# Attention of a decoder trunk: two heads to a task, score products over 128 rows, value products of both heads in turn

## The chip, the cores and the metric

One core of a Trainium2 chip. The time is device microseconds of one execution; the kernel before has a median of 2147.78 us over three runs (2141.76 to 2147.9).

## What is computed

Two layers, each a half-step SwiGLU FFN, a mixer, a second FFN and a gated per-layer embedding, on 512 positions of 1024 features in f32. The mixer projects its input to q, k, v (8 heads of 64) and to the input of a state-space branch (SSM); attention and SSM outputs are normalised, joined and projected. Cut to the attention, with the three dilated windows as one masked softmax:

```python
proj = rms_norm(h, mix_pre_g[i]) @ w_in[i]
q, k, v, u = jnp.split(proj, [D_ATTN, 2 * D_ATTN, 3 * D_ATTN], axis=-1)
q, k = partial_rotary(q, positions), partial_rotary(k, positions)
attn = dilated_mixture_attention(q, k, v)     # per head: softmax(q k^T / 8 + mask) v
ssm = s5_mixer(u, ...)
mixed = jnp.concatenate([rms_norm(attn, attn_norm_g[i]), rms_norm(ssm, ssm_norm_g[i])], -1)
h = h + rms_norm(mixed @ w_out[i], mix_post_g[i])
```

The mask is the logarithm of the number of windows that hold a key (0, 1, 2 or 3), so that one softmax over the causal keys gives the mixture.

## The kernel before

Activations lie transposed (128 features on the partitions, 512 positions in a row). Dense products keep f32 precision with three float32r products each: weights and inputs are split into a high and a low part on ScalarE (a copy) and VectorE (a difference), and high*high, high*low, low*high are added in PSUM (`mm3`). Weights stream from HBM by SyncE's queue in units of up to 128x1024 words and are split just ahead of use.

The order of all instructions is fixed when the program is built. A planner (`Clock`) keeps a model of when each engine, tile and bank is free; generators (`spawn`) for attention, SSM lanes, weight splits and normalisations yield until their inputs are due, and whenever PE would have to wait, or between two steps of three dense products, the planner lets those that are due issue their instructions (`tick`). So each engine's queue is an interleaving; on the chip it is run strictly in that order. All PE products are recorded at line 562 (`mm`), transposes at 568 (`flip`), and the other engines' operations at 353. A tile named `sb_all`, `sr_all` or `z` is a large SBUF area cut into slots of 512 words (`sr_all` in float32r, 36 slots); `ps_all` is PSUM with 8 banks of 512 words.

The mixer (`mix`, lines 1732 to 1830) projects u and the first q/k pair, then v, starts two SSM lanes (`mixer`) and `attention`, projects the other q/k tiles while those run, then the SSM gate (`glu`), the SSM half of the output projection, and last, when attention is complete, the attention half (`finish`).

Attention goes over t = 0..3, a pair of heads each, since 128 partitions hold two heads of 64. `parts` (1663) makes from q and k of the pair: per head a tile with the high part of q on its own 64 partitions and the low part on the other 64, and a tile with the high part of k on both halves; and one tile `kl`, shared, with the low parts of k, each head's on its own half. Then for each block of 128 queries (qi = 3, 2, 1, 0) and each head, `head` (1620) is one task, at most LIVE = 6 at a time:

- two score products of W = 128 (qi + 1) keys into one PSUM bank: 128 rows (high and low q, high k) at line 1639 and 64 rows (high q, low k) at line 1640;
- VectorE adds the mask and takes the row maximum (a custom operation), ScalarE the exponential with its sum, VectorE a reciprocal and a scaling;
- qi + 1 transposes into a bank, and a copy to SBUF by ScalarE;
- qi + 1 value products with 64 weight columns, f32, into the head's half of the partitions of a bank that the eight tasks of t share (line 1658). On the chip an f32 product is two instructions, so four such products are eight records.

`attended` (1709) waits for the eight tasks, then scales and splits the result for `finish`.

Of the kernel before, what the change touches and what calls it, by code (L numbers as in the profile page):

```python
# [10 lines left out]
F32 = mybir.dt.float32  # L11
# [5 lines left out]
P = 128  # L17
SEQ = 512
# [33 lines left out]
LIVE = 6  # L52
# [683 lines left out]
class Trunk(Kernel):  # L736
# [886 lines left out]
    def head(self, M, t, hh, qi, bank):  # L1623

        v = M["v"]
        q, k, kl = (self.r(b) for b in M["parts"][t][hh])
        n = qi + 1
        W = n * P
        rows = slice(hh * HD, (hh + 1) * HD)
        yield self.ck.ready(q, k, kl[rows])  # L1630
        while len(self.sl.free) < 2:
            yield self.ck.after(200.0)
        p, pt = self.sl.get(), self.sl.get()
        st = self.o_st + 2 * (self.nst % 32)
        self.nst += 1
        m, den = self.w(st, 1), self.w(st + 1, 1)
        bk = yield from self.tbank()
        c = slice(qi * P, (qi + 1) * P)
        self.mm(self.pb(bk, W), q[:, c], k[:, 0:W], True, False)
        self.mm(self.pb(bk, W), q[rows, c], kl[rows, 0:W], False, True)  # L1640
        self.ve.tensor_tensor_reduce(
            out=self.b(p, W), in0=self.pb(bk, W), in1=self.w(self.o_const + C_MASK + SEQ - W, W), scale=-1.0,
            scalar=3e38, op0=ALU.add, op1=ALU.min, accum_out=m)
        self.free(bk)
        self.act(self.b(p, W), self.b(p, W), AF.Exp, scale=-1.0, bias=m, accum_out=den)
        yield self.ck.ready(self.b(p, W))
        self.ve.reciprocal(den, den)
        self.ts(self.b(p, W), self.b(p, W), den)
        yield self.ck.ready(self.b(p, W))
        bk = yield from self.tbank()  # L1650
        for j in range(n):
            self.flip(self.pb(bk, P, j * P), self.b(p)[:, j * P:(j + 1) * P])
        self.act(self.b(pt, W), self.pb(bk, W))
        self.free(bk)
        self.sl.put(p)
        yield self.ck.ready(self.b(pt, W))
        for j in range(n):
            self.mm(self.ps[rows, bank * SEQ + qi * P:bank * SEQ + (qi + 1) * P],
                    self.b(v[j])[:, t * P + hh * HD:t * P + (hh + 1) * HD], self.b(pt)[:, j * P:(j + 1) * P],
                    j == 0, j == n - 1)  # L1660
        self.sl.put(pt)
# [284 lines left out]
```

## Time and profile before

| | us |
|---|---|
| median of three runs | 2147.78 |
| the profiled execution's own time | 2144.88 |
| its span, first to last instruction | 2143.1 |
| PE busy | 2090.1 |
| VectorE busy | 1334.3 |
| ScalarE busy | 798.4 |

The two mixers' attention lies between 470 and 614 us and between 1533 and 1670 us of the span. Times in views are counted from the span's start. A matmul's length in a view is its modelled flight time; in a stream they overlap, so what one costs is the distance from its start to the next one's start. A merged row of the timeline shows the shape of its first instruction: the score rows at 525 and 604 hold 128-row and 64-row products in turn.

### The profile page before, as it was taken

How to read it: one execution, taken by the hardware profiler on the slowest of the kernel's cores; microseconds unless marked ns; L12 is line 12 of the kernel's file. 1: busy time of each engine (PE TensorE's matmuls, PEld its weight loads, DVE VectorE, ACT ScalarE, POOL GpSimd, SP SyncE). 2: the span in 40 equal slices, each digit the busy share in tenths (PEclk: the TensorE clock that was granted, in tenths of full speed). 3: DMA queues.
4: the chain of work that ended last, by engine and by line, in shares of the span. 5: the costliest groups of instructions: out<-in, count | busy, mean ns of one | idle time of the engine just before them, and what ended most of it. 6: DMA issues, size and time to landing. Idle time of an engine off the chain costs nothing.

```text
span 2143.1 us, 30766 instructions
## 1 busy us (share of the span) xinstructions
PE 2090.1 (98%) x11936; PEld 1780.0 (83%) x11936; DVE 1334.3 (62%) x2516; ACT 798.4 (37%) x1406; POOL 156.1 (7%) x167
## 2 busy tenths in 40 slices
PE   8999999989999999999999999998999999999997
PEld 7888888967789888889998888898777898888897
DVE  5887745776768975446674444467666864444474
ACT  4422333435554322223543222234356533222242
POOL 0000000101120000001200000011011200000022
PEclk9999999999999999999999999999999999999999
DMA  4424434471133534324324233246511333323131
GB/s 157 129 82 152 137 104 138 133 171 40 60 109 113 166 121 125 111 63 154 102 82 148 72 102 114 62 165 141 138 50 50 131 116 110 117 61 127 59 131 67
DMA packets 118145, 236.29 MB, mean 110 GB/s; under 512 B 27120, under 2 KB 58480, under 8 KB 118000
## 3 DMA queue, kind: packets, MB, share of 16 engines
q1 hardware_dynamic: 118000, 234.34, 35.3%
q8 instruction: 93, 1.52, 0.3%
q14 instruction: 52, 0.43, 0.1%
HBM read 208.60 MB, written 25.69 MB: 109 GB/s over the span
## 4 chain that ended last, share of the span: by engine, by line
PE 89%; DVE 6%; DMA 1%; issue 1%; ACT 1%; POOL 1%; SPq 0%; POOLq 0%; ACTq 0%; DVEq 0%
PE ps_all L562 88%; DVE sb_all L353 4%; DVE sr_all L353 2%; PE ps_all L568 1%; DMA sb_all<-scratch_t 1%; ACT sb_all L353 1%; POOL sb_all L353 1%; SPq L353 0%; ACT sr_all L353 0%; DVE z L353 0%; DMA sb_all<-weights 0%; DMA sb_all<-scratch_g 0%; DMA scratch_u<-sb_all 0%; ACT z L353 0%; POOLq L353 0%
## 5 line engine op out<-in xcount | busy, mean ns | idle before, releaser
L562 PE MATMUL ps_all<-sr_all 128*128 128x512 f32 (+2 forms) x7118 | 1447.2, 358 | 16.1 <-ACT sr_all L353 8.6
L562 PEld LDWEIGHTS ps_all<-sr_all 128*128 128x128 f32 (+1 forms) x7118 | 1185.1, 191 | 222.6 <-issue 19.2
L353 ACT ACTIVATE sr_all<-sb_all 128x512 fp32r<-128x512 f32 (+5 forms) x567 | 410.5, 742 | 562.7 <-DVE sb_all L353 398.9
L562 PE MATMUL ps_all<-sr_all,z 128*128 128x512 f32 (+1 forms) x2898 | 572.3, 348 | 0.9 <-DVE sr_all L353 0.9
L353 DVE TENSOR_TENSOR sr_all<-sb_all,sr_all 128x1024 fp32r<-128x1024 f32 (+5 forms) x455 | 417.8, 927 | 184.8 <-ACT sr_all L353 182.5
L562 PEld LDWEIGHTS ps_all<-sr_all,z 128*128 128x128 f32 x2898 | 469.8, 190 | 67.9 <-issue 1.8
L353 DVE TENSOR_TENSOR sb_all<-ps_all,sb_all 128x512 f32<-128x512 f32 (+1 forms) x396 | 244.4, 622 | 367.4 <-PE ps_all L562 361.7
L353 ACT ACTIVATE sb_all<-sb_all 128x256 f32<-128x256 f32 (+3 forms) x390 | 188.6, 490 | 483.2 <-DVE sb_all L353 481.1
L353 POOL TENSOR_TENSOR sb_all<-sb_all 128x256 f32<-128x256 f32 (+3 forms) x159 | 152.3, 960 | 1982.1 <-ACT sb_all L353 1739.1
L353 DVE TENSOR_TENSOR sb_all<-sb_all 128x256 f32<-128x256 f32 (+7 forms) x597 | 233.7, 407 | 22.6 <-DMA scratch_t<-sb_all 7.9
L353 ACT ACTIVATE sb_all<-ps_all 128x512 f32<-128x512 f32 (+5 forms) x228 | 102.9, 466 | 204.5 <-PE ps_all L562 166.8
L353 DVE SCALAR_TENSOR_TENSOR sb_all<-sb_all 128x512 f32<-128x512 f32 (+4 forms) x194 | 115.8, 599 | 65.0 <-ACT sb_all L353 63.3
L353 DVE TENSOR_TENSOR z<-sb_all,z 128x1024 fp32r<-128x1024 f32 (+2 forms) x112 | 120.2, 1075 | 55.3 <-ACT z L353 55.2
L562 PE MATMUL ps_all<-sb_all 128*64 128x128 f32 (+6 forms) x1412 | 127.4, 268 | 27.2 <-DMA sb_all<-scratch_t 12.6
L562 PEld LDWEIGHTS ps_all<-sb_all 128*64 128x64 f32 (+3 forms) x1412 | 108.1, 156 | 53.2 <-issue 27.1
L353 ACT ACTIVATE z<-sb_all 128x1024 fp32r<-128x1024 f32 (+2 forms) x112 | 103.5, 926 | 58.7 <-PE ps_all L562 39.2
L353 DVE TENSOR_SCALAR sb_all<-sb_all 128x32 f32<-128x32 f32 (+7 forms) x147 | 44.1, 306 | 37.3 <-POOL sb_all L353 20.7
L353 DVE SCALAR_TENSOR_TENSOR sb_all<-sb_all,ps_all 128x256 f32<-128x256 f32 x132 | 63.1, 480 | 4.3 <-PE ps_all L562 4.2
L353 DVE SCALAR_TENSOR_TENSOR sr_all<-sb_all,sr_all 128x256 fp32r<-128x256 f32 x96 | 51.8, 549 | 0.2 <-ACT sr_all L353 0.2
L353 DVE CUSTOM_DVE_ANT_0 sb_all<-ps_all,sb_all 128x512 f32<-128x512 f32 (+3 forms) x62 | 28.4, 485 | 34.5 <-PE ps_all L562 30.6
L568 PE MATMUL ps_all<-sb_all 128*128 128x128 f32 x218 | 33.9, 274 | 0.0
L568 PEld LDWEIGHTS ps_all<-sb_all 128*128 128x128 f32 x218 | 26.4, 140 | 7.3 <-issue 1.4
(38 smaller groups left out, 170.3 us busy)
## 6 DMA issues: line engine op xcount, KB each, us to landing
sb_all<-weights SPq DMA_DIRECT2D x263, 512.0 KB, 3.7
sb_all<-weights SPq DMA_DIRECT2D x96, 320.0 KB, 2.9
scratch_t<-sb_all SPq DMA_DIRECT2D x40, 256.0 KB, 3.2
scratch_h<-sb_all SPq DMA_DIRECT2D x80, 128.0 KB, 1.7
sb_all<-scratch_h SPq DMA_DIRECT2D x40, 256.0 KB, 5.8
sb_all<-scratch_t SPq DMA_DIRECT2D x16, 512.0 KB, 6.3
sb_all<-weights SPq DMA_DIRECT2D x32, 192.0 KB, 2.3
sb_all<-xt SPq DMA_DIRECT2D x16, 128.0 KB, 3.7
```

Of the source, the lines that this page charges most:

```text
L353: return f(*a, **k)
L562: self.nc.tensor.matmul(out, lhsT, rhs, start=start, stop=stop)
L568: self.nc.tensor.transpose(out, x, self.ident)
```

## The change

`head` becomes `block`, one task for both heads of a pair and one block of queries, LIVE = 3 of them at a time.

- The second score product runs over all 128 rows: `parts` now makes a low tile of k per head and copies it to the other half (two more copies on ScalarE for each t, and six `sr_all` slots in place of five), so the product holds also low q times low k.
- Where two heads' scores fit in one bank (qi = 0 and 1), they share it, as do their transposes, and one copy evacuates both; otherwise a task takes two banks and four slots.
- A value product of one head and one of the other stand in turn; their outputs are the two halves of the partitions of the same bank.
- The planner counts value products at half their former cost (`share` = 2).

```diff
@@ -49,7 +49,7 @@
 HEAD = 6
 PLE_HEAD = 4
 GLU_AT = 4
-LIVE = 6
+LIVE = 3
 LANES = ((0, 1), (2, 3))
 PREP_AT = 35000.0
@@ -1620,70 +1620,95 @@
         self.tt(dst, dst, self.b(b), ALU.add, eng=self.po)
         self.sl.put(b)
-    def head(self, M, t, hh, qi, bank):
+    def block(self, M, t, qi, bank):
         v = M["v"]
-        q, k, kl = (self.r(b) for b in M["parts"][t][hh])
+        parts = [[self.r(b) for b in x] for x in M["parts"][t]]
         n = qi + 1
         W = n * P
-        rows = slice(hh * HD, (hh + 1) * HD)
-        yield self.ck.ready(q, k, kl[rows])
-        while len(self.sl.free) < 2:
+        one = 2 * W <= SEQ
+        yield self.ck.ready(*[x for p in parts for x in p])
+        need = 2 if one else 4
+        while len(self.sl.free) < need:
             yield self.ck.after(200.0)
-        p, pt = self.sl.get(), self.sl.get()
-        st = self.o_st + 2 * (self.nst % 32)
-        self.nst += 1
-        m, den = self.w(st, 1), self.w(st + 1, 1)
-        bk = yield from self.tbank()
+        bufs = [self.sl.get() for _ in range(need)]
+        p = [self.b(bufs[0])[:, hh * W:(hh + 1) * W] if one else self.b(bufs[hh], W) for hh in range(2)]
+        pt = [self.b(bufs[1])[:, hh * W:(hh + 1) * W] if one else self.b(bufs[2 + hh], W) for hh in range(2)]
         c = slice(qi * P, (qi + 1) * P)
-        self.mm(self.pb(bk, W), q[:, c], k[:, 0:W], True, False)
-        self.mm(self.pb(bk, W), q[rows, c], kl[rows, 0:W], False, True)
-        self.ve.tensor_tensor_reduce(
-            out=self.b(p, W), in0=self.pb(bk, W), in1=self.w(self.o_const + C_MASK + SEQ - W, W), scale=-1.0,
-            scalar=3e38, op0=ALU.add, op1=ALU.min, accum_out=m)
-        self.free(bk)
-        self.act(self.b(p, W), self.b(p, W), AF.Exp, scale=-1.0, bias=m, accum_out=den)
-        yield self.ck.ready(self.b(p, W))
-        self.ve.reciprocal(den, den)
-        self.ts(self.b(p, W), self.b(p, W), den)
-        yield self.ck.ready(self.b(p, W))
-        bk = yield from self.tbank()
+        bks = []
+        sc = []
+        for hh in range(2):
+            if not (one and hh):
+                bks.append((yield from self.tbank()))
+            sc.append(self.pb(bks[-1], W, W * hh if one else 0))
+        for (q, k, kl), s in zip(parts, sc):
+            self.mm(s, q[:, c], k[:, 0:W], True, False)
+            self.mm(s, q[:, c], kl[:, 0:W], False, True)
+        dens = []
+        for hh in range(2):
+            st = self.o_st + 2 * (self.nst % 32)
+            self.nst += 1
+            m, den = self.w(st, 1), self.w(st + 1, 1)
+            dens.append(den)
+            self.ve.tensor_tensor_reduce(
+                out=p[hh], in0=sc[hh], in1=self.w(self.o_const + C_MASK + SEQ - W, W), scale=-1.0,
+                scalar=3e38, op0=ALU.add, op1=ALU.min, accum_out=m)
+            self.act(p[hh], p[hh], AF.Exp, scale=-1.0, bias=m, accum_out=den)
+        self.free(*bks)
+        for hh in range(2):
+            yield self.ck.ready(p[hh])
+            self.ve.reciprocal(dens[hh], dens[hh])
+            self.ts(p[hh], p[hh], dens[hh])
+        yield self.ck.ready(*p)
+        bks = []
+        for hh in range(2):
+            if not (one and hh):
+                bks.append((yield from self.tbank()))
+            for j in range(n):
+                self.flip(self.pb(bks[-1], P, (W * hh if one else 0) + j * P), p[hh][:, j * P:(j + 1) * P])
+            if not one:
+                self.act(pt[hh], self.pb(bks[-1], W))
+        if one:
+            self.act(self.b(bufs[1], 2 * W), self.pb(bks[0], 2 * W))
+        self.free(*bks)
+        self.sl.put(*bufs[:need // 2])
+        yield self.ck.ready(*pt)
         for j in range(n):
-            self.flip(self.pb(bk, P, j * P), self.b(p)[:, j * P:(j + 1) * P])
-        self.act(self.b(pt, W), self.pb(bk, W))
-        self.free(bk)
-        self.sl.put(p)
-        yield self.ck.ready(self.b(pt, W))
-        for j in range(n):
-            self.mm(self.ps[rows, bank * SEQ + qi * P:bank * SEQ + (qi + 1) * P],
-                    self.b(v[j])[:, t * P + hh * HD:t * P + (hh + 1) * HD], self.b(pt)[:, j * P:(j + 1) * P],
-                    j == 0, j == n - 1)
-        self.sl.put(pt)
+            for hh in range(2):
+                rows = slice(hh * HD, (hh + 1) * HD)
+                self.mm(self.ps[rows, bank * SEQ + qi * P:bank * SEQ + (qi + 1) * P],
+                        self.b(v[j])[:, t * P + hh * HD:t * P + (hh + 1) * HD], pt[hh][:, j * P:(j + 1) * P],
+                        j == 0, j == n - 1, 2)
+        self.sl.put(*bufs[need // 2:])
     def parts(self, M, t):
         q, k = self.b(M["q"][t]), self.b(M["k"][t])
-        got = yield from self.rs.tgets(1, 1, 1, 1, 1)
-        kl = self.r(got[4])
-        heads = [(self.r(got[2 * hh]), self.r(got[2 * hh + 1])) + tuple(
+        got = yield from self.rs.tgets(1, 1, 1, 1, 1, 1)
+        heads = [tuple(self.r(g) for g in got[3 * hh:3 * hh + 3]) + tuple(
             slice(g * HD, (g + 1) * HD) for g in (hh, 1 - hh)) for hh in range(2)]
         yield self.ck.written(q)
-        for a, _, own, _ in heads:
+        for a, _, _, own, _ in heads:
             self.act(a[own], q[own])
-        yield max(self.ck.written(a[own]) for a, _, own, _ in heads)
-        for a, _, own, other in heads:
+        yield max(self.ck.written(a[own]) for a, _, _, own, _ in heads)
+        for a, _, _, own, other in heads:
             self.tt(a[other], q[own], a[own].bitcast(F32), ALU.subtract)
         yield self.ck.written(k)
-        for _, b, own, _ in heads:
+        for _, b, _, own, _ in heads:
             self.act(b[own], k[own])
-        yield max(self.ck.written(b[own]) for _, b, own, _ in heads)
-        for _, b, own, other in heads:
-            self.tt(kl[own], k[own], b[own].bitcast(F32), ALU.subtract)
+        yield max(self.ck.written(b[own]) for _, b, _, own, _ in heads)
+        for _, b, l, own, other in heads:
+            self.tt(l[own], k[own], b[own].bitcast(F32), ALU.subtract)
             self.act(b[other], k[own])
+        yield max(self.ck.written(l[own]) for _, _, l, own, _ in heads)
+        for _, _, l, own, other in heads:
+            self.act(l[other], l[own].bitcast(F32))
         self.sl.put(M["q"][t], M["k"][t])
         M["rs"][t] = got
-        M["parts"][t] = [(got[2 * hh], got[2 * hh + 1], got[4]) for hh in range(2)]
+        M["parts"][t] = [tuple(got[3 * hh:3 * hh + 3]) for hh in range(2)]
     def attention(self, i, M):
@@ -1695,13 +1720,12 @@
             bank = yield from self.tbank()
             mine = []
             for qi in range(3, -1, -1):
-                for hh in range(2):
-                    while sum(not d[0] for d in live) >= LIVE:
-                        yield self.ck.after(100.0)
-                    d = self.ck.spawn(self.head(M, t, hh, qi, bank))
-                    live.append(d)
-                    mine.append(d)
-                    live = [d for d in live if not d[0]]
+                while sum(not d[0] for d in live) >= LIVE:
+                    yield self.ck.after(100.0)
+                d = self.ck.spawn(self.block(M, t, qi, bank))
+                live.append(d)
+                mine.append(d)
+                live = [d for d in live if not d[0]]
             ends.append(self.ck.spawn(self.attended(i, t, M, bank, mine)))
         while not all(d[0] for d in ends):
             yield self.ck.after(100.0)
```

What that makes of PE's order is shown at three places of the first mixer. In names, `sr_all` products 128x512, 128x384, 128x256 and 128x128 are dense or score products by their width (64x128 is a value or mixer product with 64 weight columns; L568 a transpose).

The scores of t = 2, behind the SSM gate's products. Before:

```order
L562 MATMUL ps_all<-sr_all 128x512 x45
L562 MATMUL ps_all<-sr_all,z_4015 128x512 x3
L562 MATMUL ps_all<-sr_all 128x512 x2
L562 MATMUL ps_all<-sr_all 128x384 x2
L562 MATMUL ps_all<-sr_all 128x256 x2
L562 MATMUL ps_all<-sr_all 128x512 x2
L562 MATMUL ps_all<-sr_all 128x384 x2
L562 MATMUL ps_all<-sr_all 128x256 x2
L562 MATMUL ps_all<-sr_all,z_4015 128x512 x15
```

and now:

```order
L562 MATMUL ps_all<-sr_all 128x512 x45
L562 MATMUL ps_all<-sr_all,z_4007 128x512 x18
L562 MATMUL ps_all<-sr_all 128x512 x4
L562 MATMUL ps_all<-sr_all 128x384 x4
L562 MATMUL ps_all<-sr_all 128x256 x4
L562 MATMUL ps_all<-sr_all,z_4007 128x512 x9
```

Each head's scores of the first three blocks were a row of their own (x2: one 128-row and one 64-row product); now both heads' four products stand together.

Value products at t = 0, where one head's tiles lie in `z`. Before:

```order
L568 MATMUL ps_all<-sb_all,z_3362 128x128 x3
L562 MATMUL ps_all<-sr_all 128x256 x2
L562 MATMUL ps_all<-z_3362,sb_all 64x128 x4
L562 MATMUL ps_all<-sr_all 128x128 x2
L562 MATMUL ps_all<-sr_all 128x512 x3
```

and now:

```order
L562 MATMUL ps_all<-sb_all 64x128
L562 MATMUL ps_all<-z_3362,sb_all 64x128
L562 MATMUL ps_all<-sb_all 64x128
L562 MATMUL ps_all<-z_3362,sb_all 64x128 x5
L562 MATMUL ps_all<-sr_all 128x512 x3
L562 MATMUL ps_all<-sr_all 128x128 x4
```

Four products of one head in a row have become products of two heads in turn.

The end of attention, ahead of the attention half of the output projection (128x256). Before:

```order
L562 MATMUL ps_all<-sr_all 128x128 x2
L562 MATMUL ps_all<-sr_all,z_4015 128x512 x3
L568 MATMUL ps_all<-sb_all 128x128 x2
L562 MATMUL ps_all<-sr_all,z_4015 128x512 x3
L568 MATMUL ps_all<-sb_all 128x128 x2
L562 MATMUL ps_all<-sr_all,z_4015 128x512 x3
L568 MATMUL ps_all<-sb_all 128x128
L562 MATMUL ps_all<-sr_all,z_4015 128x512 x3
L562 MATMUL ps_all<-sb_all 64x128 x2
L568 MATMUL ps_all<-sb_all 128x128
L562 MATMUL ps_all<-sb_all 64x128 x4
L562 MATMUL ps_all<-sr_all 128x256 x21
```

and now:

```order
L562 MATMUL ps_all<-sb_all 64x128 x8
L562 MATMUL ps_all<-sr_all 128x256 x4
L562 MATMUL ps_all<-sb_all 64x128 x6
L562 MATMUL ps_all<-sr_all,z_4007 128x512 x3
L562 MATMUL ps_all<-sr_all 128x128 x4
L568 MATMUL ps_all<-sb_all 128x128 x6
L562 MATMUL ps_all<-sb_all 64x128 x6
L562 MATMUL ps_all<-sr_all 128x256 x18
```

Before, four times three dense products stood between the last scores (128x128 x2) and the last value products; now the last scores are followed directly by the last transposes.

## Rows read from the trace of the kernel before

**Rows 1.** Span and mean granted TensorE clock of the one core.
```profile
core 0: 2143.1 us, clock 0.988
```

**Rows 2.** Part 1 of the page: busy time, share of the span, instructions.
```profile
PE 2090.1 (98%) x11936; PEld 1780.0 (83%) x11936; DVE 1334.3 (62%) x2516; ACT 798.4 (37%) x1406; POOL 156.1 (7%) x167
```

**Rows 3.** Part 4 of the page: the chain that ended last, by engine.
```profile
PE 89%; DVE 6%; DMA 1%; issue 1%; ACT 1%; POOL 1%; SPq 0%; POOLq 0%; ACTq 0%; DVEq 0%
```

**Rows 4.** Busy time by stretch: us, engines' busy (instructions), clock, DMA share, GB/s.
```profile
470.00:541.00 71.00, 68.24 (x483) 50.33 (x480) 48.96 (x117) 37.57 (x77) 10.76 (x7) 0.95 0.18 49
541.00:569.00 28.00, 27.74 (x134) 20.54 (x133) 23.23 (x37) 14.77 (x28) 4.66 (x3) 1.00 0.15 48
569.00:614.00 45.00, 44.11 (x237) 32.19 (x238) 26.39 (x77) 29.36 (x69) 3.50 (x3) 1.00 0.22 71
...
1620.00:1670.00 50.00, 50.00 (x252) 36.58 (x251) 31.28 (x83) 32.63 (x75) 6.51 (x4) 0.97 0.17 54
```

**Rows 5.** Group by line, engine, shape: the 64-row product of the widest score.
```profile
L562 PE MATMUL ps_all<-sr_all 64*128 64x512 f32 x16 | 8.2, 514 | 0.0
```

**Rows 6.** Score products on PE: start us, us, engine, line, form, count.
```profile
525.12 4.41 PE L562 MATMUL ps_all<-sr_all 128*128 128x512 f32 x12
529.46 0.74 PE L562 MATMUL ps_all<-sr_all,z 128*128 128x512 f32 x2
...
604.45 0.58 PE L562 MATMUL ps_all<-sr_all 128*128 128x128 f32 x2
604.96 0.96 PE L562 MATMUL ps_all<-sr_all,z 128*128 128x512 f32 x3
```

**Rows 7.** Dense products on PE, undisturbed stretches.
```profile
514.13 10.48 PE L562 MATMUL ps_all<-sr_all 128*128 128x512 f32 x45
524.44 0.85 PE L562 MATMUL ps_all<-sr_all,z 128*128 128x512 f32 x3
...
659.59 4.48 PE L562 MATMUL ps_all<-sr_all 128*128 128x256 f32 x36
```

**Rows 8.** Products with 64 weight columns on PE: mixer (465), values (580, 1638).
```profile
465.22 1.09 PE L562 MATMUL ps_all<-sb_all 128*64 128x128 f32 x16
466.25 0.98 PE L562 MATMUL ps_all<-sb_all,z 64*64 64x128 f32 x14
...
580.52 1.09 PE L562 MATMUL ps_all<-sb_all 128*64 128x128 f32 x8
581.54 0.44 PE L568 MATMUL ps_all<-sb_all 128*128 128x128 f32 x2
...
1638.97 2.18 PE L562 MATMUL ps_all<-sb_all 128*64 128x128 f32 x18
1641.08 0.96 PE L562 MATMUL ps_all<-sr_all 128*128 128x512 f32 x3
1641.97 1.20 PE L562 MATMUL ps_all<-sb_all 128*64 128x128 f32 x9
```

**Rows 9.** Group on ScalarE by shape: copies of half a q or k.
```profile
L353 ACT ACTIVATE sr_all<-sb_all 64x512 fp32r<-64x512 f32 x48 | 30.1, 627 | 16.2 <-POOL sb_all L353 15.6
```

**Rows 10.** VectorE: first and last step of one head's 128-column softmax.
```profile
607.33 0.29 DVE L353 CUSTOM_DVE_ANT_0 sb_all<-ps_all,sb_all 128x128 f32<-128x128 f32 x1
...
608.64 0.29 DVE L353 TENSOR_SCALAR sb_all<-sb_all 128x128 f32<-128x128 f32 x1
```

**Rows 11.** The chain in order of time: start us, us, what.
```profile
541.70 0.60 ACT sb_all L353
...
568.99 8.47 PE ps_all L562 x34
...
1564.58 0.60 ACT z L353
...
1571.43 17.68 PE ps_all L562 x62
```

**Rows 12.** Busy time by stretch, columns as in rows 4.
```profile
470.00:500.00 30.00, 27.24 (x289) 20.04 (x285) 18.68 (x52) 14.20 (x29) 0.00 (x0) 0.89 0.21 52
```

## The prediction

> **What bounds the kernel now.** I looked first at the core's span and clock: 2143.1 us at 0.988 of the full clock [rows 1], so there is nearly no throttling to win. The page's first part has TensorE busy 98% of the span, the others 62% and less [rows 2], and the chain that ended last runs 89% through PE [rows 3]. Both say that PE's queue sets the time; but a busy PE is not an efficient one, since a matmul's modelled flight covers what it waits for inside the array. So the question for each stretch is what a product costs from its start to the next one's. The busy time by stretch [rows 4] shows where attention runs (470 to 614 us in the first mixer, and 1620 to 1670 at the end of the second): PE is busy there nearly throughout, VectorE 59 to 83%, ScalarE 53 to 65%. PE binds, but in one stretch VectorE is near.
>
> Two kinds of product stand out. A 64-row score product of 512 columns is in flight 514 ns and no other covers it: 16 of them add 8.2 us of busy time [rows 5]. And f32 products with 64 weight columns cost either 109 or 55 ns a record, by whether neighbours write the same half of the partitions (below).
>
> **Scores, saved 22 us.** For one t, six of the eight 128-row/64-row pairs (two heads, 512, 384 and 256 columns) stand together from 525.12 to 529.46: 4.34 us. A 128-column pair takes 604.96 - 604.45 = 0.51 us [rows 6], two of them 1.02. That is 5.36 us for a t, and with four t in two layers 42.9 us. Now all are 128-row products, as the dense ones are: 45 dense products of 512 columns take 524.44 - 514.13 = 10.31 us, 0.229 each; 36 of 256 take at most 4.48 us, 0.124 each [rows 7]. 384 columns I put halfway, 0.176. No undisturbed 128-column product of this type is in the trace; it lies between half the 256-column one (0.062) and the whole (0.124), and I take the upper end. Four of each: 4 x (0.229 + 0.176 + 0.124 + 0.124) = 2.61 us for a t, 20.9 us in all. Saved: 42.9 - 20.9 = 22.0 us (24 with the lower end).
>
> A 64-row product stands alone in the array: 16 of 512 columns are busy 8.2 us in sum [rows 5], twice and more a dense product's 0.229, because a 128-row product follows each. A rule speaks against the change here: the Trainium skill (TensorEngine Tiling, When to Use Tiling) has it that a contraction of 64 rows should use row tiling, which may double the speed. By that rule the scores would lose 5 us instead of saving 22 (third rival). The trace disagrees with it for this order of products.
>
> **Changes of the array's shape, saved 8 us.** A value run of 8 records takes 581.54 - 580.52 = 1.02 us, one of 18 records 1641.08 - 1638.97 = 2.11 us: 0.109 a record and 0.148 a run. Three dense products between two value runs take 1641.97 - 1641.08 = 0.89 us [rows 8] instead of 3 x 0.229 = 0.69: 0.20 more. So a run costs about 0.35 us beside its work. Counted in the order of PE's instructions, runs of full-height, 64-column products with 128 moving columns fall from 51 to 34: 17 x 0.35 = 6.0 us. A score pair leaves a like trace on the product behind it; 25 times that is a dense product or a transpose, at half of the 0.20 us: 2.5 us. Sum 8.5.
>
> **Value products in turn, saved 16 us.** 160 products are 320 records; alone 0.109 each. The mixer's products already alternate between the two halves: 16 records take 466.25 - 465.22 = 1.03 us [rows 8], less 0.148 for the run 0.88, or 0.055 each. The new order alternates everywhere: 320 x 0.054 = 17.3 us. In 11 places two heads' runs already touched (0.1 us each), so 16. The worst case is no overlap, 0 (the halves share a bank, but so do the mixer's); the best 17.3.
>
> Sum of PE's time: 22.0 + 8.5 + 16 = **46.5 us**, 23 a mixer.
>
> **What it adds.** Sixteen copies of half a k tile, at 627 ns [rows 9] 10 us of ScalarE; eight fewer evacuations a layer by shared banks. ScalarE has 15.6 us free of 45 in the tightest first-mixer stretch [rows 4]; a pair of heads can start 0.6 us later, which projection products on PE cover. If that cover were gone it would be 8 x 0.63 = 5 us. A large task takes two banks and four slots at once; three of them hold as many as six heads did. The numbers of instructions on PE, VectorE, ScalarE, POOL and SyncE are otherwise the same (VectorE does the same maxima, reciprocals and scalings), and the weight queue's work is untouched: its units only come earlier by what PE saves. The six slots per t instead of five do not hold up the second pair: its scores keep their place behind the v projection.
>
> **What is given back, 12 us.** First, the end of attention. In the new order the last scores of a mixer are followed directly by transposes. One head's 128-column softmax goes from 607.33 to 608.93 [rows 10], 1.6 us; a pair needs one more exponential and reading (0.6 us by the same stretch), 2.2; four transposes of the block before (4 x 0.11) cover 0.4, and the block before has only three dense products itself. Queued behind the waiting transposes are the last value products and the attention half of the output projection, which all that follows waits for. I put 2.5 us a mixer, 5 in all. Everywhere else, at least 5 us of PE's work stands between a pair's scores and its transposes in the new order (28 of 32 tasks). Second, from 541.70 to 568.99 in the first mixer the chain runs in VectorE and ScalarE [rows 11], through the SSM gate's scaling and the rotary of q and k; VectorE is busy 23.2 of 28 us there [rows 4]. What PE saves there, some 4 us, turns into waiting for that chain. Third, in the second mixer the SSM lanes' last steps end a wait of PE: 1564.58 to 1571.43 [rows 11], 6.9 us. PE already waits there, and a part of what it saves ahead only lengthens that wait: 3 us. Sum 12.
>
> 46.5 - 12 = 34 us. The profiled execution's own time is 2144.88, 2.9 us under the median of the runs: 2144.9 - 34 = **2111 us**.
>
> **Rivals.**
> - *PE was not the bound in most of attention* and two thirds of the saving become waits: for it speak the VectorE chain at 541 and that PE stood at a mean of 0.89 of the clock between 470 and 500 us, some of it at 1.2 instead of 2.4 GHz [rows 12], a spell that cost (1 - 0.89) x 30 = 3.3 us and that more waiting would lengthen. Against it: PE is busy 68.2 of 71 us up to 541 and 44.1 of 45 from 569, VectorE 49.0 and 26.4 [rows 4]. A third of 46.5 is 15.5: 2129 us, with 2120 to 2138 around it.
> - *Slower: the softmax of a pair becomes bare.* A task now carries two heads' chain before its first transpose. If PE waits for it in every task, 32 x 2.2 = 70 us come against 46.5: 2168 us. It decides from 46.5 / 32 = 1.45 us a task. For it speaks the end of attention; against it the 5 us and more in the other 28 tasks.
> - *Two 64-row products side by side*: each head's low product uses one half of the rows, and if the array runs both heads' at once, 64 of them cost half of 16 x (0.229 + 0.176 + 0.124 + 0.124) = 10.4 us, 5.2, and 128-row products in their place 10.4. Then scores lose 5.2 us where I book 22, and 46.5 - 27.2 - 12 = 7 us remain: 2138 us. The busy sum of rows 5 speaks against it. (This is what the Trainium skill's rule in TensorEngine Tiling, When to Use Tiling, would make of it.)
> - *All cover lost in the new order's other places*, within 6 us of no change: 2139 to 2151. That the change would not do what it says is excluded by the order: the counts of array-shape changes on PE fall from 277 to 123.
> - *Less is given back*, and earlier ends in one stretch pull the next: 46.5 us whole give 2098.
>
> **How the numbers follow.** My forecast, gains of 24 to 42 us (2103 to 2121), has 0.60; more than that 0.12; the first rival 0.16; the third 0.02; no change 0.05; slower 0.05. The range takes the forecast, the larger gain down to 2097 and the first rival up to 2134. About 0.3%, 6 us, is what a measurement of this kernel can tell from no change. Faster is 0.60 + 0.12 + 0.16 + 0.02 = 0.90, same 0.05, slower 0.05.
>
> **What would show it.** Right: no 64-row float32r products of this shape in the trace; a t's twelve score products of 512, 384 and 256 columns in 2.1 us instead of 4.3; value runs at 0.055 a record; attention's stretches shorter by 7 to 10 us each except the one with the VectorE chain; PE waits of 2 to 3 us just ahead of the attention half of the output projection. Wrong: value runs still at 0.109 a record (then 16 us are missing), or the same products in the same stretches with new PE waits for VectorE or ScalarE between scores and transposes.

## The result, and the profile after

The changed kernel takes 2117.1 us (median of four runs, 2111.9 to 2118.75) beside 2144.78 us for the kernel before on the same chip: a ratio of 0.986, 95% interval 0.984 to 0.988. That is 28 us by the medians, where 34 were forecast; its profiled execution took 2117.12 us against 2144.88, 27.8 us less. Forecast were 2111 us and a range of 2097 to 2134.

Span and clock of the changed kernel, which answer to [rows 1]:

```profile
core 0: 2115.3 us, clock 0.986
```

and, from parts 1 and 4 of its page, the busy sums [rows 2] and the chain by engine [rows 3]:

```profile
PE 2047.7 (97%) x11936; PEld 1761.6 (83%) x11936; DVE 1331.1 (63%) x2516; ACT 806.9 (38%) x1406; POOL 158.8 (8%) x167
...
PE 87%; DVE 7%; DMA 2%; ACT 1%; issue 1%; SPq 1%; POOL 1%; DVEq 0%; POOLq 0%; ACTq 0%
```

PE's busy time fell by 42.4 us, the span by 27.8: the difference, 14.6 us, is time in which PE now waits. The other engines' work hardly changed: ScalarE has 8.5 us more, VectorE 3.2 less.

**Scores.** In the timeline of PE (start us, us, engine, line, form, count), the twelve score products of t = 2 that answer to [rows 6]:

```profile
522.30 2.25 PE L562 MATMUL ps_all<-sr_all 128*128 128x512 f32 x12
524.38 2.22 PE L562 MATMUL ps_all<-sr_all,z 128*128 128x512 f32 x9
```

From start to next start 2.08 us, where before 4.34 stood; 2.1 had been forecast.

**Value products**, all four widths of one t in the same view (16, 12, 8 and 4 records; between them dense and score products):

```profile
538.04 1.09 PE L562 MATMUL ps_all<-sb_all 128*64 128x128 f32 x16
539.07 2.11 PE L562 MATMUL ps_all<-sr_all 128*128 128x512 f32 x10
541.11 0.88 PE L562 MATMUL ps_all<-sb_all 128*64 128x128 f32 x12
541.91 0.96 PE L562 MATMUL ps_all<-sr_all 128*128 128x512 f32 x3
542.81 0.66 PE L562 MATMUL ps_all<-sb_all 128*64 128x128 f32 x8
543.39 2.33 PE L562 MATMUL ps_all<-sr_all 128*128 128x512 f32 x9
...
562.71 0.44 PE L562 MATMUL ps_all<-sb_all 128*64 128x128 f32 x4
563.08 8.25 PE L562 MATMUL ps_all<-sr_all 128*128 128x512 f32 x37
```

They take 1.03, 0.80, 0.58 and 0.37 us from start to next start, together 2.78. In the kernel before one head alone took the same; beside the 1.02 us of eight records in [rows 8] stand, in its timeline:

```profile
582.61 0.87 PE L562 MATMUL ps_all<-sb_all 128*64 128x128 f32 x6
583.41 0.58 PE L562 MATMUL ps_all<-sr_all 128*128 128x128 f32 x2
583.92 0.65 PE L562 MATMUL ps_all<-sb_all 128*64 128x128 f32 x4
584.50 0.97 PE L562 MATMUL ps_all<-sr_all 128*128 128x512 f32 x3
...
595.25 0.43 PE L562 MATMUL ps_all<-sb_all 128*64 128x128 f32 x2
595.62 0.66 PE L568 MATMUL ps_all<-sb_all 128*128 128x128 f32 x4
```

0.80 us for six, 0.58 for four, 0.37 for two. In this t the second head's value products now cost nothing: 2.77 us less. Eight times that would be 22 us, but in the kernel before two heads' runs already touched in 11 places. Summed over the whole trace from start to next start, the products of this form (448 records, 128 of them the mixer's) took 48.1 us in 51 runs and now take 31.0 in 34: 17.1 us less. Each of the 17 runs that are gone also spares the 0.20 us that [rows 8] has behind a run, an estimated 3.4 us.

**New waits.** The idle time over 0.5 us ahead of PE's rows (in brackets, with what ended it), from 500 us of the first mixer and 1540 us of the second up to the attention half of the output projection, in the timeline of the changed kernel:

```profile
537.46 0.66 PE L568 MATMUL ps_all<-sb_all 128*128 128x128 f32 x4 [1.40 <-DVE sb_all L353]
557.10 5.67 PE L562 MATMUL ps_all<-sr_all 128*128 128x512 f32 x17 [3.41 <-ACT sr_all L353]
597.97 1.72 PE L568 MATMUL ps_all<-sb_all 128*128 128x128 f32 x6 [4.10 <-DVE sb_all L353]
603.48 1.22 PE L562 MATMUL ps_all<-sr_all 128*128 128x256 f32 x8 [0.68 <-DVE sr_all L353]
...
1550.91 0.33 PE L568 MATMUL ps_all<-sb_all 128*128 128x128 f32 x1 [0.69 <-DVE sb_all L353]
1554.79 0.44 PE L562 MATMUL ps_all<-sb_all 128*64 128x128 f32 x4 [1.48 <-ACT sb_all L353]
1601.64 16.55 PE L562 MATMUL ps_all<-sr_all 128*128 128x512 f32 x60 [3.52 <-ACT sr_all L353]
1642.30 1.72 PE L568 MATMUL ps_all<-sb_all 128*128 128x128 f32 x6 [2.98 <-DVE sb_all L353]
1647.80 0.86 PE L562 MATMUL ps_all<-sr_all 128*128 128x256 f32 x5 [0.64 <-DVE sr_all L353]
```

In the kernel before these were such waits in the same stretches:

```profile
613.76 1.58 PE L562 MATMUL ps_all<-sr_all 128*128 128x256 f32 x11 [0.89 <-DVE sr_all L353]
...
1571.43 0.43 PE L562 MATMUL ps_all<-sb_all 128*64 128x128 f32 x2 [1.61 <-ACT sb_all L353]
1671.63 1.58 PE L562 MATMUL ps_all<-sr_all,z 128*128 128x256 f32 x11 [0.89 <-DVE sr_all L353]
```

18.9 us against 3.4: 15.5 us are given back, close to the 14.6 that PE's idle time grew by on the whole span. 6.6 of them stand at the ends of attention (597.97 and 603.48, 1642.30 and 1647.80, less 0.89 each), 8.9 in the stretches of the gate (the other five rows, less 1.61). The busy time by stretch (columns as in [rows 4]) shows who is late there:

```profile
523.00:557.00 34.00, 29.25 (x173) 23.64 (x171) 30.50 (x64) 19.47 (x42) 10.37 (x6) 1.00 0.21 63
557.00:590.00 33.00, 32.87 (x186) 26.06 (x186) 21.35 (x59) 26.26 (x58) 1.61 (x2) 0.95 0.23 71
590.00:604.00 14.00, 9.05 (x72) 6.97 (x72) 8.78 (x22) 8.84 (x19) 2.48 (x2) 0.88 0.31 106
```

From 523 to 557 VectorE is busier than PE (30.50 against 29.25 of 34 us); the next 33 us are PE's again.

At 590 to 604 neither is busy throughout. VectorE's own timeline there shows why:

```profile
594.58 0.75 DVE L353 SCALAR_TENSOR_TENSOR sr_all<-ps_all,sb_all,sr_all 128x512 fp32r<-128x512 f32 x1 [1.87 <-ACT sb_all L353]
595.25 1.78 DVE L353 TENSOR_TENSOR sr_all<-sb_all,sr_all 128x1024 fp32r<-128x1024 f32 x1
596.96 0.28 DVE L353 CUSTOM_DVE_ANT_0 sb_all<-ps_all,sb_all 128x128 f32<-128x128 f32 x1
...
597.56 0.35 DVE L353 TENSOR_SCALAR sb_all<-sb_all 128x256 f32<-128x256 f32 x1
```

The last scores end at 593.9 us. Their row maxima (the custom operation) start at 596.96, since two operations stand ahead in VectorE's queue: the low part of the finished t = 2 (`attended`), itself waiting 1.87 us for ScalarE, and the low part of a weight. The transposes that PE waits for are first those of the 256-key block; their scaling (597.56) stands behind the same two operations and behind these maxima.

The clock takes a little more. In the last two stretches the granted clock is 0.95 and 0.88, where the kernel before has 1.00 from 541 to 614 [rows 4]; from 470 to 500 us it is 0.94 against 0.89 [rows 12]. As one less the clock, times the stretch, that is 3.3 and 1.8 us now and 3.3 before: by this estimate some 2 us more in the first mixer. In the second (1495 to 1650 us, before 1507 to 1673) both have 0.97.

### The profile page after: what moved, and what is told of

It is laid out like the page before. It is cut to its first block, busy times and chain, and to the rows that moved or that the text cites. A ratio compares the mean times of both kernels' runs of the same rounds, so it can differ in the third digit from the quotient of the medians.

```text
span 2115.3 us, 30750 instructions
## 1 busy us (share of the span) xinstructions
PE 2047.7 (97%) x11936; PEld 1761.6 (83%) x11936; DVE 1331.1 (63%) x2516; ACT 806.9 (38%) x1406; POOL 158.8 (8%) x167
## 3 DMA queue, kind: packets, MB, share of 16 engines
q8 instruction: 93, 1.52, 0.3%
## 4 chain that ended last, share of the span: by engine, by line
PE 87%; DVE 7%; DMA 2%; ACT 1%; issue 1%; SPq 1%; POOL 1%; DVEq 0%; POOLq 0%; ACTq 0%
PE ps_all L562 86%; DVE sb_all L353 4%; DVE sr_all L353 2%; PE ps_all L568 1%; DMA sb_all<-scratch_t 1%; ACT sb_all L353 1%; SPq L353 1%; ACT sr_all L353 1%; DVE z L353 1%; POOL sb_all L353 1%; DMA scratch_u<-sb_all 0%; DMA sb_all<-weights 0%; DMA sb_all<-scratch_u 0%; DMA sb_all<-scratch_g 0%; ACT z L353 0%
## 5 line engine op out<-in xcount | busy, mean ns | idle before, releaser
L562 PE MATMUL ps_all<-sr_all 128*128 128x512 f32 (+2 forms) x7100 | 1413.1, 355 | 22.8 <-ACT sr_all L353 16.2
L562 PEld LDWEIGHTS ps_all<-sr_all 128*128 128x128 f32 x7100 | 1176.5, 191 | 208.4 <-ACT sr_all L353 17.4
L562 PE MATMUL ps_all<-sr_all,z 128*128 128x512 f32 (+1 forms) x2916 | 580.3, 349 | 0.0
L562 PEld LDWEIGHTS ps_all<-sr_all,z 128*128 128x128 f32 x2916 | 476.4, 190 | 68.4 <-issue 1.5
L562 PE MATMUL ps_all<-sb_all 128*64 128x128 f32 (+6 forms) x1408 | 110.0, 266 | 26.1 <-DMA sb_all<-scratch_t 13.2
L562 PEld LDWEIGHTS ps_all<-sb_all 128*64 128x64 f32 (+3 forms) x1408 | 94.1, 154 | 47.7 <-issue 23.7
L353 DVE TENSOR_SCALAR sb_all<-sb_all 128x32 f32<-128x32 f32 (+8 forms) x145 | 44.6, 314 | 33.4 <-POOL sb_all L353 20.4
L568 PE MATMUL ps_all<-sb_all 128*128 128x128 f32 x216 | 33.3, 284 | 9.2 <-DVE sb_all L353 9.2
L568 PEld LDWEIGHTS ps_all<-sb_all 128*128 128x128 f32 x216 | 26.3, 143 | 16.8 <-DVE sb_all L353 11.1
```

What stands on the lines that cost most here:

```text
L353: return f(*a, **k)
L562: self.nc.tensor.matmul(out, lhsT, rhs, start=start, stop=stop)
L568: self.nc.tensor.transpose(out, x, self.ident)
```

## Experiments

All ratios are to the kernel before, run beside each on the same chip; 0.001 is 2.1 us. The changed kernel stands at 0.986 (0.9861). An interval reaches about 0.002 to either side, so two kernels of this study are clearly apart from some 6 us on. PE's idle time, the span less PE's busy time on the page of the profiled execution, is 53.0 us in the kernel before and 67.6 in the changed one.

**The pieces of the change.** First the rows. In `block`, for the blocks of 512 and 384 keys alone:

```diff
-        for (q, k, kl), s in zip(parts, sc):
+        for hh, ((q, k, kl), s) in enumerate(zip(parts, sc)):
...
-            self.mm(s, q[:, c], kl[:, 0:W], False, True)
+            rows = slice(0, P) if one else slice(hh * HD, (hh + 1) * HD)
+            self.mm(s, q[rows, c], kl[rows, 0:W], False, True)
```

This leaves out low q times low k there, as the kernel before did.

> The changed kernel, with the second score product of the two wide blocks (512 and 384 keys) back on the head's own 64 rows; the narrow blocks, whose two heads share a bank, keep 128 rows. No other instruction moves on any engine. My theory (a 64-row float32r product stands alone in the array): six pairs of a t took 4.34 us before and 2.12 as 128-row products, 2.22 less; two of the three widths are 2/3 to 0.78 of that (by count or by columns), 1.5 to 1.7 us a t, 12 to 14 us in all: 2129 to 2131 against 2117. Rival 'the rows do not matter once both heads stand together': 0 us. Rival 'two 64-row products run side by side': up to 3 us faster.

Measured: 0.9909 (0.9889 to 0.993), 10 us slower than the changed kernel; span 11.2 us more. The same twelve products in its timeline:

```profile
524.97 3.81 PE L562 MATMUL ps_all<-sr_all 128*128 128x512 f32 x12
528.62 2.24 PE L562 MATMUL ps_all<-sr_all,z 128*128 128x512 f32 x9
```

3.65 us against 2.08: 1.57 a t, 0.39 for each of the four 64-row products, 12.6 us in all, the 12 to 14 expected; the time shows 10. Both rivals fall.

Then the order of the value products, all else in place:

```diff
-        for j in range(n):
-            for hh in range(2):
+        for hh in range(2):
+            for j in range(n):
```

> The changed kernel, with the value products of a task one head after the other instead of in turn (the two loops swapped; the planner's count is kept, so nothing else moves). My theory: 320 records at 0.109 us instead of 0.055, 16 us slower (11 if some of it hides in waits that are there now): 2128 to 2134. Rival 'the alternation is worth nothing, the gain was in the shared runs': 0 us. In the trace a value run of both heads should take 0.109 us a record again.

Measured: 0.9889 (0.9868 to 0.9911), 6 us slower, about a third of what I expected, and the interval overlaps that of the changed kernel. The rows are clearer:

```profile
539.01 1.58 PE L562 MATMUL ps_all<-sb_all 128*64 128x128 f32 x16
540.53 2.09 PE L562 MATMUL ps_all<-sr_all 128*128 128x512 f32 x10
542.55 1.14 PE L562 MATMUL ps_all<-sb_all 128*64 128x128 f32 x12
543.62 0.98 PE L562 MATMUL ps_all<-sr_all 128*128 128x512 f32 x3
544.53 0.66 PE L562 MATMUL ps_all<-sb_all 128*64 128x128 f32 x8
545.13 2.34 PE L562 MATMUL ps_all<-sr_all 128*128 128x512 f32 x9
```

1.52 us for 16 records (1.03 in turn, 2.04 as two runs of the kernel before), 1.07 for 12 (0.80; 1.60), 0.60 for 8 (0.58; 1.16). So it is not 0.109 us a record again: where two heads' runs touch, about half a microsecond of the second is done beside the first. The four-record task has nothing to swap (0.37). Taking the heads in turn saves 0.78 us a t, 6 us in all. Summed over the trace as above, the products of this form take 37.1 us here: of the 17.1 us, 11.0 come from joining the two heads' runs and 6.1 from taking them in turn.

The kernel before with 128 rows alone:

```diff
-        self.mm(self.pb(bk, W), q[rows, c], kl[rows, 0:W], False, True)
+        self.mm(self.pb(bk, W), q[:, c], kl[:, 0:W], False, True)
```

and with `parts` as in the change.

> The kernel before, with only its second score product made a 128-row one (the low tile of k per head, copied to the other half, as in the change); one head to a task, value products one head after the other. The planner puts some of the order elsewhere. My theory: 22 us less of PE, of which up to a third goes to waits: 14 to 22 us faster than before, 2123 to 2131. Rival 'most of the gain comes from pairing': 0 to 5 us. Rival 'the 16 added copies cost': not faster.

Measured: 0.9941 (0.992 to 0.9963), 12.7 us faster than the kernel before, a little under the lower end, though the interval reaches into the range. The rows bring a good part of the gain without pairs, and if they are worth 22 us there too, some 9 of them are given back. PE's idle time says the same: 61.9 us, 8.9 more than before.

Both edits of the first two experiments at once, what is left being the pairs and the 128 rows of the narrow blocks:

> The changed kernel with both edits undone: 64 rows for the low products of the wide blocks, value products one head after the other. What is left of the change is the pairing (shared banks, LIVE = 3) and 128 rows in the narrow blocks. If the parts add: 12 to 14 plus 11 to 16 slower than the changed kernel, 23 to 30 us: 2140 to 2147, so within 5 us of the kernel before: what pairing saves in array-shape changes (6) and in narrow scores (some 9) is what it gives back in waits (about 14). Rival 'the parts overlap, each fills waits that the other opens': under 20 us, and the pairing alone is a gain of 8 us or more. Rival 'pairing is a loss by itself': slower than 2150.

Measured: 0.9945 (0.9927 to 0.9964), 18 us slower than the changed kernel and 12 us faster than the one before. The two parts add within the noise (10 and 6 are 16), but what is left is no zero: the rival that gave it 8 us and more had the number, though not the reason, since the parts add. Joined runs are worth 11 us and what stands behind them, where I had put 6. Two parts of the change were not taken back by themselves: LIVE = 3 and the planner's halved count of value products.

**Two 64-row products as neighbours.** The wide blocks in the order high, high, low, low, the low ones on 64 rows each (low q times low k left out again):

```diff
+                self.nc.tensor.matmul(s, q[:, c], k[:, 0:W], start=True, stop=False)
...
+        for hh, ((q, k, kl), s) in enumerate(zip(parts, sc)):
+            rows = slice(hh * HD, (hh + 1) * HD)
+            if not one:
+                self.nc.tensor.matmul(s, q[rows, c], kl[rows, 0:W], start=False, stop=True)
```

> As the kernel with 64 rows for the low products of the wide blocks, but with the two heads' low products next to each other (high, high, low, low, in two banks), one on the lower and one on the upper half of the rows; all else in the order of the changed kernel. Theory (row tiles run side by side when nothing of full height stands between): the two low products take the time of one, 0.23 + 0.18 us less for a t, 3 us faster than the changed kernel at best, and 2 to 3 us slower if each switch of shape costs 0.2: 2114 to 2120, against 2127 with the old order of these products. Rival (each 64-row product stands alone whatever its neighbour): as slow as with the old order, 10 us slower than the changed kernel.

Measured: 0.9885 (0.9869 to 0.9902), 5 us slower than the changed kernel and 5 faster than with the old order, though its interval overlaps both of theirs. Its rows (1651 and 1657 are the high and the low products) are clearer:

```profile
523.02 0.61 PE L1651 MATMUL ps_all<-sr_all 128*128 128x512 f32 x2
523.56 0.50 PE L1657 MATMUL ps_all<-sr_all 64*128 64x512 f32 x2
523.99 0.62 PE L1651 MATMUL ps_all<-sr_all 128*128 128x384 f32 x2
524.54 0.45 PE L1657 MATMUL ps_all<-sr_all 64*128 64x384 f32 x2
524.92 0.73 PE L562 MATMUL ps_all<-sr_all 128*128 128x256 f32 x4
525.49 2.25 PE L562 MATMUL ps_all<-sr_all,z 128*128 128x512 f32 x9
```

The twelve products take 2.47 us. The two 64-row products of a block start 3 ns apart in the trace (4 ns at 384 columns): they do run side by side. One reading fits this and the first experiment. Each change between 64 and 128 rows costs 0.2 us, as [rows 8] had it for the value runs, and two 64-row neighbours take the time of one. The old order has eight such changes in the wide blocks of a t: 1.6 us, 1.57 measured. The new has four, 0.8, and saves one product of 512 columns and one of 384, 0.229 + 0.176: 0.39, and 2.47 - 2.08 = 0.39. At these lengths the changes cost twice what the tiles save.

The Trainium skill (TensorEngine Tiling (Array Packing), When to Use Tiling) has it that a contraction of 64 should use 2x row tiling. This trace agrees that two such tiles work at once when they are neighbours, 3 ns apart; at these lengths it does not agree that they pay. The Trainium skill (the same page, Tiling Modes, Key Properties) also has it that a change of the tiling mode drains the engine. The 0.2 us a change are in line with that.

**What is given back.** The wait at the end of attention: one more task at a time, so that in the planned order dense products stand between the last scores and their transposes.

```diff
-LIVE = 3
+LIVE = 4
```

> The changed kernel with LIVE = 4: the 128-key block of the last pair is let in one task earlier, so that in the planned order some 30 dense products stand between the last scores of the first mixer and their transposes, where none stood. My theory: the wait of 4.1 us there (3.0 in the second mixer) and the two short ones behind it, some 8 us more than before the change, mostly go: 5 to 8 us faster than the changed kernel, 2109 to 2112 on the scale of 2117. Rival 'VectorE's queue is simply full at the end, the wait only moves behind the scores of another block': within 2 us. Rival 'a fourth task holds banks and slots that the projections need': slower by 2 to 5 us.

Measured: 0.9868 (0.9853 to 0.9883), no gain. The waits of 4.10 and 2.98 us at the end are gone from its timeline (the short ones behind them stay, 0.68 and 0.89), but these have come:

```profile
548.91 0.69 PE L568 MATMUL ps_all<-sb_all 128*128 128x128 f32 x2 [6.02 <-DVE sb_all L353]
...
1594.12 0.69 PE L568 MATMUL ps_all<-sb_all 128*128 128x128 f32 x2 [4.82 <-ACT sb_all L353]
```

They stand in the stretch of the gate, where VectorE was already full: the wait moved. PE's idle time is 69.1 us, no less than in the changed kernel. Then the gate's chain, its four tiles scaled in one go (in `glu`):

```diff
-                self.split(self.r(h), self.r(l), self.b(t))
-                self.sl.put(t, ys[n])
-                xs.append((h, l))
-                yield self.ck.idle("DVE", 1000.0)
+                self.act(self.r(h), self.b(t))
+                self.sl.put(ys[n])
+                got.append((t, h, l))
+            for t, h, l in got:
+                self.tt(self.r(l), self.b(t), self.r(h).bitcast(F32), ALU.subtract)
+                self.sl.put(t)
+                xs.append((h, l))
```

> The changed kernel, with the four tiles of the normalised SSM output scaled and copied one behind the other and their low parts taken after that, instead of tile by tile with other work of VectorE between. My theory: PE's waits for this chain ahead of the SSM half of the output projection (3.4 us in the first mixer, 3.8 in the second, 0.8 each behind them) go, 4 to 7 us faster than the changed kernel: 2110 to 2113. Rival 'what stood between the tiles, the rotary and the softmax, is late instead': within 2 us.

Measured: 0.9839 (0.9818 to 0.986), 5 us faster by the ratio, but its interval overlaps that of the changed kernel (0.9844 to 0.9878). The profiled execution, the slowest of its four (2119.3 us, the others 2110.1 to 2114.8), has a span of 2117.5 us and so none of the gain, but its waits are shorter: PE's idle time is 60.4 us, 7.2 less than in the changed kernel. The wait ahead of the last transposes is not in its timeline either, since the planner's order moved, and a wait of 2.65 us for VectorE stands ahead of the SSM half in the second mixer, where 3.52 stood. In the time this stays unclear; in the waits it is what was expected. Both together:

> Both edits. If the two waits are separate, the gains add: 9 to 14 us faster than the changed kernel, 2103 to 2108. If both only wait for the same full VectorE queue: no better than the better of the two alone.

Measured: 0.9806 (0.9788 to 0.9824), 2107.6 us, 12 us faster than the changed kernel, as expected, and by the ratios more than the sum of the two alone (none and 5). That the fourth task pays once the gate's chain doesn't stand in its way would explain it, but the waits don't show it: PE's idle time is 59.7 us with both edits and 60.4 with the gate's alone. What makes both some 7 us faster than that one (the two intervals just overlap) is not in the waits and stays open. What is left of the wait is 2.8 us ahead of the last 18 transposes in each mixer, and from 530 to 565 us both engines are nearly full:

```profile
530.00:565.00 35.00, 33.35 (x182) 26.30 (x180) 32.85 (x58) 25.10 (x44) 7.31 (x4) 1.00 0.23 75
```

With `GLU_AT = 6` in addition, the gate two projections later:

> The kernel with LIVE = 4 and the gate's scaling first, with the gate moved two projections later (GLU_AT = 6), so that the scores of t = 2 come before the gate's products. What is left there of PE's waits that end with VectorE or ScalarE are 2.8 us ahead of the last 18 transposes of each mixer. Theory: VectorE gets the softmax of t = 2 and the gate's chain apart, and these waits shrink: 2 to 5 us faster than that kernel, 2102 to 2106 on the scale of 2117 for the changed one. Rival: two projections less stand between the gate and the SSM half of the output projection, and its chain is bare again: slower by 3 to 6 us.

Measured: 0.9793 (0.9779 to 0.9808), 2104.1 us, the fastest kernel of the study: 14.6 us below the changed one, 44 below the one before. Its lead over the last (0.9806) is 2.8 us, within the 2 to 5 expected, but the intervals overlap, and the reason expected is not borne out: the two waits of 2.8 us are gone, others have come (2.31 us at 556.35, 5.30 at 1592.78), and PE's idle time, 60.8 us, is no less than the last kernel's.

Last, the queue itself: LIVE = 3 and the old gate, but `attended` and the low parts of weights held back from the scores of the last 256-key block until the last pair is scaled:

```diff
         yield self.ck.ready(ps)
+        while M.get("tail"):
+            yield self.ck.after(100.0)
```

(and the same wait ahead of a weight's low part in `splitter`, which until then splits only the unit that is needed next).

> The changed kernel (LIVE = 3, gate as it was), with VectorE's queue at the end of attention put otherwise: the low part of the finished t = 2 and the weight split that stand ahead of the last pair's softmax come behind it. PE's order up to the attention half of the output projection is the same. My theory (the wait of 4.1 us is the queue, not the softmax itself): the last maxima start at once after the scores instead of 3.1 us later, the wait ahead of the last transposes of the first mixer is 1.2 to 2 us, and what moved back costs little: 2 to 4 us faster over both mixers, 2113 to 2115. Rival (the chain of the pair's softmax is that long): wait still over 3.5 us, no gain. Rival (what moved is late for the output projection): the wait comes back there, no gain.

Measured: 0.9906 (0.9879 to 0.9932), 9.7 us slower. The place itself did what the theory says:

```profile
595.00 1.58 PE L568 MATMUL ps_all<-sb_all 128*128 128x128 f32 x6 [1.18 <-DVE sb_all L353]
...
601.29 1.85 PE L562 MATMUL ps_all<-sr_all 128*128 128x256 f32 x8 [1.76 <-DVE sr_all L353]
```

The wait of 4.10 us is 1.18; so 2.9 of it were the queue, and the softmax of a pair is no longer than priced. But 1.76 us stand as a wait for the low parts that were held, where the changed kernel has 0.68, and from 605 to 610 us the granted clock is 0.66 where the changed kernel has 1.00. By the products of the norm behind the output projection (634.36 us against 633.49) the kernel is 0.9 us behind. The profiled execution is 12.6 us longer in its span, so most of the loss lies after the first mixer, and not in waits: PE's idle time is 68.7 us, 1.1 more. The granted clock from 1430 us to behind the second mixer's attention is 0.95 (to 1710 us) against 0.97 (to 1700): one less the clock, times the stretch, is 14 us against 8, an estimated 6 of the 12.6. The planner also put weight splits elsewhere; what the rest comes from was not followed up.

## Why the prediction was right, and where it was off

The forecast was right in sign and mechanism, and the time lay in the range.

- *Scores, 22 us*: right. Six pairs of a t came to 2.08 us (2.1 forecast), 18.1 us in all. The 128-key products stand in the ten of 539.07: 2.04 us less six dense ones (1.37) leaves 0.67 for four, a change of shape in it, against 0.50 forecast and 1.02 before: 3 to 4 us. Sum 21 to 22. What the 64 rows cost is the two changes of shape around each, 0.2 us apiece, rather than the length of the product; for the order as it was that is the same number. The prediction set the 514 ns of [rows 5], which are flight, beside 0.229 us from start to start; from start to start such a product took 0.43 us, the change behind it included.
- *Changes of shape 8.5 and value products 16*: too much by some 4 us, and parted wrongly. The value runs gave 17.1 us and, by estimate, 3.4 behind them: 20.5 where 6.0 and 16 had been booked. The second experiment turns the shares round: 11 for joining the two heads' runs, 6 for taking them in turn. The step that was off is "The new order alternates everywhere: 320 x 0.054", less 0.1 us for each of the 11 places where runs touched: it credits the turn with what touching alone gives, and that is half a microsecond. The remaining 2.5 us, behind the score pairs, found no row.
- *Gross 46.5*: 21 to 22 and 20.5, so some 42.
- *Given back, 12*: too little; the waits say 15.5. The end of attention, 5 forecast, is 6.6. The term was built from the softmax of a pair, and that was right; what it left out is what else VectorE's queue holds then. The gate's chain in the first mixer, 4 forecast, is 4.8. The third term, 3 us of longer waiting for the SSM lanes at 1571, fell: the wait in that place, now at 1554.79, is 1.48 against 1.61. The gate's chain shows in the second mixer as in the first (5.7 in three rows with that one, less 1.61). The 2 us of clock in the first mixer were not in this term.

So of the missing 6 us 3.5 are waits; the rest lies with PE and the clock and can't be parted: 42 less 15.5 and 2 would be 24.5 us, and 27.8 were measured, so some 3 us of the saving stand in no row. Of the rivals, the one that turned two thirds of the saving into waits had the right cause for half as much, a third. That the pair's softmax is bare in every task did not come: the longer waits are the nine shown, and two of them stand ahead of a mixer's last transposes. The third rival's mechanism exists, two 64-row neighbours do run at once, but with its changes of shape that order is slower than 128 rows by 0.39 us a t. The range's lower end, all of 46.5 kept, was not reached by this kernel.

## What to carry to other kernels

Count the changes of PE's array shape, not only its products: products of two heads on different halves, joined in one run and taken in turn, cost what one head costs. When PE's work in a stretch falls below the next engine's, look at that engine's queue in order, at what stands ahead of the instruction that PE waits for. Try edits to waits in the same queue together too: here one that gained nothing alone and one that gained 5 us gave 12 together, though why is not shown. An order that is right at the wait can still be worse for the whole: what was held back was wanted next (1.76 us against 0.68), and most of that loss is not explained.

## What was not expected of the hardware

- Value products of two heads overlap without standing in turn: 16 records in two blocks of eight took 1.52 us, where in turn they took 1.03 and as separate runs 2.04. Only about half a microsecond of the second block runs beside the first. That different tiles can work in parallel is in the Trainium skill (TensorEngine Tiling (Array Packing), Tiling Modes, Key Properties), and the rows in turn agree, 16 in the time of 8. How far apart two may stand shows where one head's tiles lie in `z` and the two can be told apart: in the second experiment the second head's first record starts at 1547.64 us, with three of the first head's eight still to start; so by the trace the starts of two heads need not follow the order of the queue.
- Two 64-row neighbours of 512 columns took 0.43 us together and of 384 columns 0.38, the change of shape behind them included: the time of one such product between 128-row ones in the kernel before (0.43 and 0.37).
- In the last experiment PE was busier than in the changed kernel from 595 to 605 us (7.72 us against 6.18, the granted clock 0.83 in both), and yet the clock was 0.66 for another 5 us of unbroken work, so for a part of it 1.2 instead of 2.4 GHz, where the changed kernel had 1.00.
